# Order and padding of SBUF tiles in a two-layer decoder trunk in float32r

## The chip, the cores and the metric

The kernel runs on one core of a Trainium2 chip. The metric is the device time of one execution in microseconds (us). A core has a matrix engine (TensorE: PE in the profile, PEld for its weight loads), VectorE (DVE), ScalarE (ACT), GpSimd (POOL) and SyncE (SP); data come from HBM by DMA into SBUF, a memory of 128 partitions, and products go to PSUM. An address below is the offset in bytes within each partition of SBUF.

## The reference

Two layers over 256 tokens of width 2,048. Layer 0 has causal attention with 16 heads (the sequence is one MoBA block, so no past blocks are gathered), layer 1 a sliding window of 128 with four shared K/V heads and sinks. Each layer then has a gated FFN with a causal convolution of width 3, and each half ends in a layer norm over a scaled residual.

```python
def conv_ffn(x, w_up, conv_w, conv_b, w_down):
    h = x @ w_up                                   # [256, 2 * 5504]
    hc = conv_width_3(h, conv_w) + conv_b
    g, v = jnp.split(hc, 2, axis=-1)
    return (jax.nn.gelu(g) * v) @ w_down
...
for layer in range(2):
    attn = moba_attention(...) if layer == 0 else swa_attention(...)
    h = layer_norm(ALPHA * h + attn, ln_g[layer, 0], ln_b[layer, 0])
    ffn = conv_ffn(h, ffn_w_up[layer], ffn_conv_w[layer], ffn_conv_b[layer], ffn_w_down[layer])
    h = layer_norm(ALPHA * h + ffn, ln_g[layer, 1], ln_b[layer, 1])
```

Everything is float32.

## The kernel before

**Products in two parts.** A float32 operand is split into a high part in float32r and a low part, the rest (L84 and L85 for weights: ACT copies `raw` to `wh`, DVE subtracts to `wl`). A product is then three float32r products: high with high, high with low, low with high. Activations are kept in the same way, both parts in one tile: a block `k` of `xT`, `oT` or `aT` has 512 columns, the high part of 256 tokens and then the low part.

**The stream of weights.** All weights come as one stream of 709 halves of [128, 1024] float32, 512 KB each, in the order of use. `load_weights` (L65) issues a load on SP into one of four `raw` buffers, `split_upto` (L73) splits a half into one of four pairs `wh`/`wl`, three halves ahead of the products.

**Two kinds of products.** `ws_unit` (L194) makes a [128 features, 256 tokens] tile: per block of 128 rows, 128 columns of `wh` are stationary and all 512 columns of `xT[:, k]` move (L223), then 128 columns of `wl` are stationary and the 256 columns of the high part move (L224). It serves Q and K and the FFN's up-projection (86 units in each FFN, of which the first has another form, L207 to L212, with only 256 columns moving). `Moving` (L227) has 128 columns of the activations stationary, and a block of 512 columns of weights moves (L243 to L245): V, the attention's output projection (`src` is `oT`) and the FFN's down-projection (`aT`). All these products are float32r. Attention itself (L384, L385, L418, L419 and the transposes L411) and the transposes L324 are float32.

**Weights in xT.** In the last window of each `project_out`, xT is free, and four halves of weights (`aside`, L77 to L79) are split into xT instead of `wh`/`wl`: there both parts of a moving block are pieces of xT, 2,048 bytes long.

**Places.** A pool takes its place when it is opened, and a tile's buffers follow each other within it in the order of the calls, each rounded up to 32 bytes. The first 16,512 bytes hold the DMA ring and four constants. Then come `const` (L50: xT at 16,512, res, ident, eps, sk, nsk, junk), `wpool` (raw from 66,368), `spool` (wh from 82,752, wl from 99,136), `stat` (L55: small tiles, four buffers each, and `stats`), `gbp` (gb at 116,608), and from 132,992 on the pool of the stage, `att0`, `ffn0`, `att1` or `ffn1`, each opened when the one before is closed. In `att0` the order is xc, rb, oh, us, bias, oT (170,432), vt, qT, kT, L, PT; in `att1` bias, oT (149,376), vt, kT, qT, L, PT; in an FFN aT (132,992), cw, c0, c1, h. The pools end below 229,376, which is the end of a partition.

**Order of the work.** It is written out by hand: `at(n, f)` puts f ahead of the products of the n-th slot (a half) from now, `pe_at` behind them. SP's queue has the weight loads, POOL's the small loads, among them `cw` (L511), `band` and `bias` (L188, L192) and `gb` (L293); `layer_attention` (L435) sets the loads of bias to slots 4 and on.

Of the kernel before, what the change touches and what calls it, by code (L numbers as in the profile page):

```python
# [11 lines left out]
F32 = mybir.dt.float32  # L12
F32R = mybir.dt.float32r
# [4 lines left out]
P = 128  # L18
T = 256
D = 2048  # L20
KB = D // P
NH = 16
# [4 lines left out]
NCH = D // 512  # L27
# [3 lines left out]
ALPHA = math.sqrt(2.0)  # L31
# [15 lines left out]
def trunk(ctx: ExitStack, tc: tile.TileContext, wst, xT_in, x_in, relb, onehot, umask, sinks, conv_in, ln_g, ln_b, out):  # L47
    nc = tc.nc
    ctx.enter_context(tc.manual_schedule())
    const = ctx.enter_context(tc.tile_pool(name="const", bufs=1))  # L50
    wpool = ctx.enter_context(tc.tile_pool(name="wpool", bufs=RAW_BUFS))
    spool = ctx.enter_context(tc.tile_pool(name="spool", bufs=HALF_BUFS))
    psum = ctx.enter_context(tc.tile_pool(name="psum", bufs=4, space=bass.MemoryType.PSUM))
    dram = ctx.enter_context(tc.tile_pool(name="dram", bufs=1, space=bass.MemoryType.DRAM))
    stat = ctx.enter_context(tc.tile_pool(name="stat", bufs=4))  # L55
    gbp = ctx.enter_context(tc.tile_pool(name="gbp", bufs=1))

    n_halves = wst.shape[0]
    raws, halves, aside = {}, {}, {}
# [13 lines left out]
    def split_upto(i):  # L73
        while todo["split"] <= min(i, n_halves - 1):
            s = todo["split"]
            r = raws.pop(s)
            if s in aside:  # L77
                j = aside.pop(s)
                wh, wl = (xT[:, k:k + 2, :].rearrange("p a b -> p (a b)") for k in (4 * j, 4 * j + 2))  # L79
            else:  # L80
                wh = spool.tile([P, HW], F32R, name="wh")
                wl = spool.tile([P, HW], F32R, name="wl")
            for c in pieces(s):
                nc.scalar.activation(wh[:, c], r[:, c], AF.Copy)  # L84
                nc.vector.tensor_tensor(out=wl[:, c], in0=r[:, c], in1=wh[:, c].bitcast(F32), op=ALU.subtract)  # L85
            halves[s] = (wh, wl)
            todo["split"] += 1
            load_weights()

    slot = {"now": 0}  # L90
    before, behind = {}, {}

    def at(n, f, *a, first=False):
        """f runs n slots (halves of a unit of weights) from now, ahead of that slot's products."""
        fs = before.setdefault(slot["now"] + n, [])
        fs.insert(0 if first else len(fs), (f, a))

    def pe_at(n, f, *a):
        """f runs n slots from now, behind that slot's products."""
        behind.setdefault(slot["now"] + n, []).append((f, a))  # L100

    def run(agenda):
# [4 lines left out]
    def step():  # L107
        run(behind)
        slot["now"] += 1
# [3 lines left out]
    def take(ahead=AHEAD):  # L113
        i = nexth["i"]
        nexth["i"] += 1
        split_upto(i + ahead)
        run(before)
        return halves.pop(i)

    xT = const.tile([P, KB, 2 * T], F32R, name="xT")  # L120
    res = const.tile([P, 2, D], F32, name="res")

    def load_input(pool):
        xc = pool.tile([P, KB, T], F32, name="xc", bufs=1)
# [67 lines left out]
        nc.gpsimd.dma_start(bias[:, h0:h1, :], band[l, h0:h1].rearrange("h q j -> q h j"))  # L192

    def ws_unit(acc, feed=None):  # L194
        """acc[:, :T] += acc[:, T:] is x @ w, transposed. With feed, acc[:, :T] alone, with the
        products with the low part of x last: feed(k) readies the high part of block k, feed(KB)
        the low parts."""
        def cols(w, j):
            return w[:, j * P:(j + 1) * P]

        o = acc[:, 0:T]
        if feed:
            pair = [take(1 - i) for i in range(2)]
            for k in range(KB):
                feed(k)
                wh, wl = pair[k // 8]
                nc.tensor.matmul(o, cols(wh, k % 8), xT[:, k, 0:T], start=(k == 0), stop=False)  # L207
                nc.tensor.matmul(o, cols(wl, k % 8), xT[:, k, 0:T], start=False, stop=False)
            feed(KB)
            split_upto(nexth["i"] + AHEAD - 2)  # L210
            for k in range(KB):
                nc.tensor.matmul(o, cols(pair[k // 8][0], k % 8), xT[:, k, T:2 * T], start=False, stop=(k == KB - 1))  # L212
                if k % 8 == 7:
                    step()
                    split_upto(nexth["i"] + AHEAD - 2 + (k + 1) // 8)
                    if k < 8:
                        run(before)
            return
        for hf in range(2):
            wh, wl = take()  # L220
            for j in range(8):
                k = hf * 8 + j
                nc.tensor.matmul(acc, cols(wh, j), xT[:, k, :], start=(k == 0), stop=False)  # L223
                nc.tensor.matmul(o, cols(wl, j), xT[:, k, 0:T], start=False, stop=(k == KB - 1))  # L224
            step()

    class Moving:  # L227
        """Products with the weights as the moving operand, block after block of [128, 512]."""

        def __init__(self, src, nk):  # L230
            self.src, self.nk, self.half, self.pos = src, nk, None, 0
# [13 lines left out]
            nc.tensor.matmul(acc, sl, wh, start=False, stop=(k == self.nk - 1))  # L245

        def tilewise(self, accs, k, n, done):
            """Blocks k .. k+n, all of which the buffers hold, for one token tile after the other;
            done(t, i) is called behind half i of tile t."""
            blocks = []  # L250
            for t in range(2):
                for i in range(n):
                    if t == 0:
                        blocks.append(self.block(min(AHEAD, n // 2 - 1 - i // 2)))
                    self.mm(accs[t], k + i, t, *blocks[i])
                    if i % 2:
                        if t:
                            step()
                        done(t, i // 2)
                        if t:  # L260
                            run(before)

        def chunk(self, accs, early=None, late=None):
            """One chunk of 512 columns; early and late are the `done` of its first and its last
            blocks, done for one token tile after the other."""
            k = 0
            if early:
                k = 2 * HALF_BUFS
                self.tilewise(accs, 0, k, early)
            last = WINDOW_BLOCKS if late else 0  # L270
            while k < self.nk - last:
                wh, wl = self.block()
                for t in range(2):
                    self.mm(accs[t], k, t, wh, wl)
                k += 1
                if self.pos % 2 == 0:
                    step()
            if late:
                self.tilewise(accs, k, last, late)
# [2 lines left out]
        return psum.tile([P, 512], F32, name="acc")  # L282

    def project_out(src, nk, li, after, preload):
        """res = layer_norm(ALPHA * res + src @ w); its transpose goes to xT, split. For tile 1 the
        last steps, over chunks of columns, are returned."""
        mv = Moving(src, nk)
        w0 = nexth["i"] + (nk * NCH - WINDOW_BLOCKS) // 2
        aside.update({w0 + j: j for j in range(SPARE)})
        stats = stat.tile([P, 2, NCH, 6], F32, name="stats", bufs=1)  # L290
        gb = gbp.tile([P, 2, D], F32, name="gb")
        for i, a in enumerate((ln_g, ln_b)):
            nc.gpsimd.dma_start(gb[:, i], bass.AP(tensor=a.tensor, offset=a.offset + li * D, ap=[[0, P], [1, D]]))  # L293
# [77 lines left out]
        return lambda c: norm(1, c), (lambda c: turn(1, c), lambda c, pt: low(1, c, pt))  # L371

    def attention(pool, l, h, qT, vt, kT, bias, oT):
        """Softmax attention of head h, from the slot after the one that completes q^T."""
        at_tile = lambda: psum.tile([P, 512], F32, name="at")
        L = pool.tile([P, 3 * P], F32, name="L", bufs=3)
        PT = pool.tile([P, 3 * P], F32, name="PT", bufs=3)
# [2 lines left out]
        tiles = ((0, slice(0, P)), (1, slice(P, 3 * P)))  # L380
# [53 lines left out]

    def layer_attention(l, rest):  # L435
        with tc.tile_pool(name=f"att{l}", bufs=2) as pool:
            if l == 0:
                load_input(pool)
                bias_table(pool)
            else:  # L440
                nc.vector.tensor_scalar(nsk, sk, -1.0, None, op0=ALU.mult)
            bias = pool.tile([P, NH, 2 * P], F32, name="bias", bufs=1)
            for i, h in enumerate(range(0, NH, 4)):
                at(4 + (8 - 4 * l) * i, spread_bias, l, h, h + 4)
                at(4 + (8 - 4 * l) * i, load_bias, bias, l, h, h + 4)
            oT = pool.tile([P, NH, 2 * T], F32R, name="oT", bufs=1)

            def v_group(early=None):
                mv = Moving(xT, KB)
# [23 lines left out]
            if l == 0:  # L473
                for g in range(NH // 4):
                    vt = v_group()
                    for j in range(4):
                        h = 4 * g + j
                        q = feat_unit("qT", 4)
                        k = feat_unit("kT", 4)
                        attention(pool, l, h, q, vt[:, :, j * P:(j + 1) * P], k, bias, oT)  # L480
            else:
# [19 lines left out]
                for h in range(NH):  # L501
                    q = feat_unit("qT", 4)
# [73 lines left out]


def _still(w):
    """[K, N] as tiles of 128 columns, in two halves of K."""
    k, n = w.shape  # L580
    return w.reshape(2, k // P // 2, P, n // P, P).transpose(3, 0, 2, 1, 4).reshape(n // P, 2, P, HW)


def _moving(w):
    """[K, N] as blocks of [128, 512], two side by side, chunk of columns after chunk."""
    k, n = w.shape
    b = w.reshape(k // P, P, n // 512, 512).transpose(2, 0, 1, 3).reshape(-1, 2, P, 512)
    return b.transpose(0, 2, 1, 3).reshape(-1, P, HW)
# [59 lines left out]
```

## Time and profile before

| | |
|---|---|
| device time, median of 3 runs (lowest, highest) | 2143.48 us (2142.07, 2143.63) |
| span of the profiled execution, first to last instruction | 2143.1 us |
| its mean granted clock | 0.993 |
| PE, PEld, DVE, ACT, POOL busy | 99%, 84%, 67%, 46%, 1% |
| moved by DMA | 405.08 MB, 189 GB/s on the mean |

The profile is one execution taken by the hardware profiler. A matmul's busy time runs from its start to a modelled end, and consecutive matmuls overlap; the distance between two starts is what one costs in a full row of them. The granted clock is TensorE's, as a share of 2.4 GHz: 1.00, or 0.50 (1.2 GHz). A stage given with its bounds has, per engine, busy us and the number of instructions. The chain of waits goes back from the last instruction to what released each one.

### The profile page before, as it was taken

The numbers are of one execution on the slowest core, as the hardware profiler recorded it, in microseconds if no ns is written. First come the engines' busy times: TensorE is split into PE (matmuls) and PEld (weight loads), VectorE is DVE, ScalarE is ACT, GpSimd is POOL, SyncE is SP. The second block draws the span as 40 slices with busy tenths as digits, with TensorE's granted clock in tenths as the row PEclk, the third lists the DMA queues.
The fourth block names the chain that finished last, engine by engine and source line by source line (L and its number), as shares of the span: only waits on it lengthen the run. The fifth ranks groups of instructions, "written<-read, shape, count | busy, mean of one in ns | idle before, by whom it ended". The sixth has DMA issues, their size and how long they took to land.

```text
span 2143.1 us, 28513 instructions
## 1 busy us (share of the span) xinstructions
PE 2113.8 (99%) x10962; PEld 1792.8 (84%) x10962; DVE 1435.0 (67%) x2104; ACT 987.6 (46%) x1395; POOL 25.5 (1%) x40
## 2 busy tenths in 40 slices
PE   8999999999999999999999999999999999999997
PEld 7888888788888888888887888888888888888886
DVE  5555555787787777744456676687787778754445
ACT  5444444354544444433344554354444454443342
POOL 1100000000000000000001000000000000000000
PEclk9999999999999999999999999999999999999999
DMA  8855556455555555555556544565555555555553
GB/s 278 295 171 174 169 167 204 174 196 189 186 188 183 188 186 187 186 188 189 189 200 201 212 147 158 176 209 188 187 187 183 190 185 185 184 190 190 187 186 128
DMA packets 114120, 405.08 MB, mean 189 GB/s; under 512 B 15504, under 2 KB 15808, under 8 KB 112704
## 3 DMA queue, kind: packets, MB, share of 16 engines
q1 hardware_dynamic: 106848, 383.83, 53.4%
q0 software_dynamic: 7136, 19.44, 2.6%
q8 instruction: 86, 1.41, 0.3%
q14 instruction: 50, 0.41, 0.1%
HBM read 401.02 MB, written 6.34 MB: 190 GB/s over the span
## 4 chain that ended last, share of the span: by engine, by line
PE 97%; DVE 2%; DMA 0%; ACT 0%; issue 0%; SPq 0%; ACTq 0%
PE acc L223 39%; PE acc L224 20%; PE acc L244 12%; PE acc L245 12%; PE acc L243 12%; PE at L385 1%; PE at L418 1%; PE at L411 0%; DVE wl L85 0%; PE at L324 0%; PE at L384 0%; DMA raw<-in_wst_dram 0%; PE at L419 0%; DVE res L315 0%; DVE res L314 0%; ACT wh L84 0%
## 5 line engine op out<-in xcount | busy, mean ns | idle before, releaser
L85 DVE TENSOR_TENSOR wl<-raw,wh 128x1024 fp32r<-128x1024 f32 (+1 forms) x709 | 865.2, 1222 | 626.0 <-ACT wh L84 625.5
L223 PE MATMUL acc<-xT,wh 128*128 128x512 f32 x3552 | 1262.4, 397 | 0.0
L84 ACT ACTIVATE wh<-raw 128x1024 fp32r<-128x1024 f32 (+1 forms) x709 | 750.4, 1059 | 953.4 <-PE acc L245 353.1
L224 PE MATMUL acc<-xT,wl 128*128 128x256 f32 x3552 | 1000.9, 282 | 0.0
L223 PEld LDWEIGHTS acc<-xT,wh 128*128 128x128 f32 x3552 | 667.6, 188 | 159.2
L224 PEld LDWEIGHTS acc<-xT,wl 128*128 128x128 f32 x3552 | 667.1, 188 | 0.9
L243 PE MATMUL acc<-wh,aT 128*128 128x512 f32 x656 | 259.7, 396 | 0.0
L245 PE MATMUL acc<-wh,aT 128*128 128x512 f32 x656 | 259.4, 395 | 0.0
L244 PE MATMUL acc<-wl,aT 128*128 128x512 f32 x656 | 259.4, 395 | 0.0
L245 PEld LDWEIGHTS acc<-wh,aT 128*128 128x128 f32 x656 | 123.3, 188 | 29.7
L243 PEld LDWEIGHTS acc<-wh,aT 128*128 128x128 f32 x656 | 123.3, 188 | 29.6
L244 PEld LDWEIGHTS acc<-wl,aT 128*128 128x128 f32 x656 | 123.3, 188 | 29.5
L243 PE MATMUL acc<-wh,oT 128*128 128x512 f32 x224 | 90.1, 402 | 0.0
L245 PE MATMUL acc<-wh,oT 128*128 128x512 f32 x224 | 88.5, 395 | 0.0
L244 PE MATMUL acc<-wl,oT 128*128 128x512 f32 x224 | 88.4, 395 | 0.0
L534 DVE SCALAR_TENSOR_TENSOR c<-h,cw,c 128x255 f32<-128x255 f32 x170 | 82.3, 484 | 6.0
L535 DVE SCALAR_TENSOR_TENSOR c<-h,cw,c 128x254 f32<-128x254 f32 x170 | 82.1, 483 | 6.1
L243 PE MATMUL acc<-wh,xT 128*128 128x512 f32 x160 | 67.1, 419 | 7.9 <-ACT wh L84 7.9
L533 DVE TENSOR_SCALAR c<-h,cw 128x256 f32<-128x256 f32 x170 | 70.3, 414 | 6.1
L532 DVE TENSOR_TENSOR h<-acc,h 128x256 f32<-128x256 f32 x170 | 70.9, 417 | 0.0
L244 PE MATMUL acc<-wl,xT 128*128 128x512 f32 x160 | 65.4, 409 | 1.5 <-DVE wl L85 1.3
L541 ACT ACTIVATE aT<-c 128x256 fp32r<-128x256 f32 x86 | 36.0, 419 | 66.4 <-DVE c L538 66.4
(102 smaller groups left out, 1199.3 us busy)
## 6 DMA issues: line engine op xcount, KB each, us to landing
raw<-in_wst_dram SPq DMA_DIRECT2D x723, 512.0 KB, 3.3
band<-ud POOLq DMA_DIRECT2D x8, 512.0 KB, 12.8
bias<-band POOLq DMA_DIRECT2D x8, 512.0 KB, 5.5
gb<-in_ln_g_dram POOLq DMA_DIRECT2D x4, 1024.0 KB, 6.3
gb<-in_ln_b_dram POOLq DMA_DIRECT2D x4, 1024.0 KB, 9.0
res<-in_x_dram POOLq DMA_DIRECT2D x2, 1024.0 KB, 9.7
out_dram<-res SPq DMA_DIRECT2D x8, 256.0 KB, 2.5
xc<-in_xT_dram SPq DMA_DIRECT2D x7, 256.0 KB, 7.4
```

What stands on the lines that cost most here:

```text
L84: nc.scalar.activation(wh[:, c], r[:, c], AF.Copy)
L85: nc.vector.tensor_tensor(out=wl[:, c], in0=r[:, c], in1=wh[:, c].bitcast(F32), op=ALU.subtract)
L223: nc.tensor.matmul(acc, cols(wh, j), xT[:, k, :], start=(k == 0), stop=False)
L224: nc.tensor.matmul(o, cols(wl, j), xT[:, k, 0:T], start=False, stop=(k == KB - 1))
L243: nc.tensor.matmul(acc, sh, wh, start=(k == 0), stop=False)
L244: nc.tensor.matmul(acc, sh, wl, start=False, stop=False)
L245: nc.tensor.matmul(acc, sl, wh, start=False, stop=(k == self.nk - 1))
L532: nc.vector.tensor_tensor(out=h, in0=acc[:, 0:T], in1=h, op=ALU.add)
L533: nc.vector.tensor_scalar(c, h, w[:, 2:3], w[:, 3:4], op0=ALU.mult, op1=ALU.add)
L534: nc.vector.scalar_tensor_tensor(c[:, 1:T], h[:, 0:T - 1], w[:, 1:2], c[:, 1:T], op0=ALU.mult, op1=ALU.add)
L535: nc.vector.scalar_tensor_tensor(c[:, 2:T], h[:, 0:T - 2], w[:, 0:1], c[:, 2:T], op0=ALU.mult, op1=ALU.add)
L541: nc.scalar.activation(aT[:, i, 0:T], g, AF.Copy)
```

## The change

Only places change, no instruction. xT and res leave `const` for a pool `big` of their own, opened behind `stat`, which moves ahead of the large pools; `stats` is padded from 6 to 10 elements per entry, 128 bytes in all; and in the attention pools oT and bias are taken first, in this order. The docstrings of several functions are blanked, with the line count kept.

```diff
     const = ctx.enter_context(tc.tile_pool(name="const", bufs=1))
+    stat = ctx.enter_context(tc.tile_pool(name="stat", bufs=4))
+    big = ctx.enter_context(tc.tile_pool(name="big", bufs=1))
     wpool = ctx.enter_context(tc.tile_pool(name="wpool", bufs=RAW_BUFS))
     spool = ctx.enter_context(tc.tile_pool(name="spool", bufs=HALF_BUFS))
     psum = ctx.enter_context(tc.tile_pool(name="psum", bufs=4, space=bass.MemoryType.PSUM))
     dram = ctx.enter_context(tc.tile_pool(name="dram", bufs=1, space=bass.MemoryType.DRAM))
-    stat = ctx.enter_context(tc.tile_pool(name="stat", bufs=4))
     gbp = ctx.enter_context(tc.tile_pool(name="gbp", bufs=1))
...
-    xT = const.tile([P, KB, 2 * T], F32R, name="xT")
-    res = const.tile([P, 2, D], F32, name="res")
+    xT = big.tile([P, KB, 2 * T], F32R, name="xT")
+    res = big.tile([P, 2, D], F32, name="res")
...
-        stats = stat.tile([P, 2, NCH, 6], F32, name="stats", bufs=1)
+        stats = stat.tile([P, 2, NCH, 6], F32, name="stats", bufs=1, padded_shape=[P, 2, NCH, 10])
...
         with tc.tile_pool(name=f"att{l}", bufs=2) as pool:
+            oT = pool.tile([P, NH, 2 * T], F32R, name="oT", bufs=1)
+            bias = pool.tile([P, NH, 2 * P], F32, name="bias", bufs=1)
             if l == 0:
                 load_input(pool)
                 bias_table(pool)
             else:
                 nc.vector.tensor_scalar(nsk, sk, -1.0, None, op0=ALU.mult)
-            bias = pool.tile([P, NH, 2 * P], F32, name="bias", bufs=1)
             for i, h in enumerate(range(0, NH, 4)):
...
-            oT = pool.tile([P, NH, 2 * T], F32R, name="oT", bufs=1)
```

## Rows read from the trace of the kernel before

**Rows 1.** The page, busy us (share of the span) xinstructions of each engine.
```profile
PE 2113.8 (99%) x10962; PEld 1792.8 (84%) x10962; DVE 1435.0 (67%) x2104; ACT 987.6 (46%) x1395; POOL 25.5 (1%) x40
```

**Rows 2.** The chain of waits, whole span, shares by line.
```profile
by line: PE acc L223 38.7%; PE acc L224 19.8%; PE acc L244 11.8%; PE acc L245 11.7%; PE acc L243 11.7%; PE at L385 0.6%; PE at L418 0.6%; PE at L411 0.5%; DVE wl L85 0.5%; PE at L324 0.4%; PE at L384 0.4%; DMA raw<-in_wst_dram 0.3%; PE at L
```

**Rows 3.** Matmul groups by line and shape: xcount | busy us, mean ns | idle before.
```profile
L223 PE MATMUL acc<-xT,wh 128*128 128x512 f32 x3552 | 1262.4, 397 | 0.0
...
L243 PE MATMUL acc<-wh,aT 128*128 128x512 f32 x656 | 259.7, 396 | 0.0
...
L243 PE MATMUL acc<-wh,oT 128*128 128x512 f32 x224 | 90.1, 402 | 0.0
...
L243 PE MATMUL acc<-wh,xT 128*128 128x512 f32 x160 | 67.1, 419 | 7.9 <-ACT wh L84 7.9
```

**Rows 4.** Timeline of PE, FFN up-projection, layer 0: start us, us; first and last.
```profile
700.16 0.28 PE L224 MATMUL acc<-xT,wl 128*128 128x256 f32 x1
...
705.81 0.28 PE L224 MATMUL acc<-xT,wl 128*128 128x256 f32 x1
```

**Rows 5.** Timeline of PE, beside attention, layer 0: first and last.
```profile
61.21 0.28 PE L224 MATMUL acc<-xT,wl 128*128 128x256 f32 x1
...
65.75 0.28 PE L224 MATMUL acc<-xT,wl 128*128 128x256 f32 x1
```

**Rows 6.** Timeline of PE, FFN down-projection, layer 0: first and last.
```profile
1060.03 0.40 PE L244 MATMUL acc<-wl,aT 128*128 128x512 f32 x1
...
1066.33 0.39 PE L244 MATMUL acc<-wl,aT 128*128 128x512 f32 x1
```

**Rows 7.** Stage (span, busy by engine, PEclk, DMA), then chain, under the lower clock.
```profile
405.00:408.00 3.00, 3.00 (x16) 3.00 (x15) 2.60 (x5) 0.67 (x2) 1.60 (x3) 0.50 0.31 46
...
405.07 0.21 PE acc L208
```

**Rows 8.** Timeline of PE, weights in xT: layer 0, then layer 1's two token tiles.
```profile
374.74 0.39 PE L243 MATMUL acc<-xT,oT 128*128 128x512 f32 x1
...
379.41 0.39 PE L245 MATMUL acc<-xT,oT 128*128 128x512 f32 x1
...
1372.85 0.39 PE L243 MATMUL acc<-xT,oT 128*128 128x512 f32 x1
...
1377.38 0.39 PE L245 MATMUL acc<-xT,oT 128*128 128x512 f32 x1
...
1384.59 0.39 PE L243 MATMUL acc<-xT,oT 128*128 128x512 f32 x1
...
1387.99 0.39 PE L243 MATMUL acc<-xT,oT 128*128 128x512 f32 x1
```

**Rows 9.** The first two of these stretches, busy us by engine, PEclk, DMA share, GB/s.
```profile
374.74:379.40 4.66, 4.66 (x21) 3.76 (x20) 4.62 (x6) 1.58 (x2) 0.00 (x0) 1.00 0.25 75
1372.85:1377.39 4.54, 4.54 (x22) 3.76 (x21) 4.51 (x6) 1.50 (x2) 0.00 (x0) 1.00 0.19 63
```

**Rows 10.** Chain of waits, first unit of each FFN, in order of time.
```profile
410.95 1.88 PE acc L212 x16
...
1408.24 1.81 PE acc L212 x16
```

**Rows 11.** One stage of the up-projection, then the page's GB/s in 40 slices.
```profile
500.00:600.00 100.00, 100.00 (x568) 87.03 (x568) 78.91 (x125) 49.90 (x71) 0.00 (x0) 1.00 0.55 184
...
GB/s 278 295 171 174 169 167 204 174 196 189 186 188 183 188 186 187 186 188 189 189 200 201 212 147 158 176 209 188 187 187 183 190 185 185 184 190 190 187 186 128
```

**Rows 12.** Timeline of POOL, then of DVE: last load of bias, first use.
```profile
1174.98 0.78 POOL L192 DMA_DIRECT2D bias<-band  x1 [16.08 <-DMA band<-ud]
...
1199.38 0.28 DVE L389 SCALAR_TENSOR_TENSOR L<-at,bias 128x128 f32<-128x128 f32 x1
```

**Rows 13.** Timeline of PE, project_out of layer 0: first and last.
```profile
340.12 0.40 PE L244 MATMUL acc<-wl,oT 128*128 128x512 f32 x1
...
345.00 0.40 PE L244 MATMUL acc<-wl,oT 128*128 128x512 f32 x1
```

## The prediction

> **What bounds the kernel now.** I read the page's busy line first, then the chain of waits by line, then the matmul groups with shapes kept apart, then start times. PE is busy for 99% of the span [rows 1], and the chain is made of the products of L223, L224 and L243 to L245 almost alone [rows 2]. So only what changes the distance from one matmul's start to the next, or what makes PE wait anew, can move the time. "Busy" does not show that distance, because matmuls overlap (L223 has a mean of 397 ns and 3,552 of them [rows 3] would be 1,410 us); start times do. Three patterns carry the time:
> - FFN up-projection, L223 (512 moving columns) and L224 (256) in turn: 16 pairs in 5.65 us, 353 ns a pair [rows 4].
> - The same pairs beside attention: 13 pairs in 4.54 us, 349 ns [rows 5].
> - L243 to L245, always 512 columns: 27 starts in 6.30 us, 233.3 ns each [rows 6].
>
> How much is that above what the columns need? While the granted clock was at its lower level (0.50, 1.2 GHz), a matmul of 256 columns took 0.21 us on the chain, 256/1.2 = 213 ns, nothing over [rows 7]. At the full clock (1.00, 2.4 GHz) the same count would be 107 ns, 512 columns 213 ns, a pair 320 ns. So a pair loses 29 to 33 ns and a 512-column product 20 ns, only at the full clock.
>
> **Does an operand's address decide that loss?** The addresses follow from the pools' order and the tiles' sizes (each rounded up to 32 bytes). Before, with the first 16,512 bytes taken, xT lies at 16,512, wh and wl from 82,752 and 99,136 on, aT at 132,992, oT at 170,432 in layer 0 and at 149,376 in layer 1. Their remainders by 128 are 0 for xT, aT and layer 1's oT, and 64 for wh, wl and layer 0's oT. The trace holds an experiment on this. Near the end of each project_out four halves of weights are put into xT instead of wh and wl, so the same code moves xT against oT in both layers. Layer 1 (remainders 0 and 0): 20 starts in 4.53 us, 226.5 ns, and for the second token tile 15 in 3.40 us, 226.7. Layer 0 (0 and 64): 20 starts in 4.67 us, 233.5 ns [rows 8]. Clock, DVE and ACT were alike beside them, and DMA was light in both [rows 9]. The products that move wh (64) against aT (0) have 233.3 [rows 6]. So where both operands start at multiples of 128 the product costs 6.6 ns less. An address does matter.
>
> It isn't all. The 16 products of L212 (256 columns) in each FFN's first unit have the same addresses in both layers, and took 1.88 us in one and 1.81 us in the other, 118 and 113 ns [rows 10]; likewise the pairs with 353 and 349 [rows 4, 5]. So the chain has states that it can fall into at one set of addresses. The best ones agree: 113.3 is half of 226.6. I take these as what aligned operands give: a pair would be 226.6 + 113.3 = 340 ns.
>
> The Trainium skill says otherwise. Its page "TensorE: Matmul & The Clock Gate", section "What happens when you issue a matmul", has TensorE read moving operand and weights through two independent ports, so that a weight load takes nothing from a running product, and by "Back-to-back issue gap" 512 columns take some 216 ns wherever they lie. By that the change gives nothing; rows 8 speak against it, 233.3 is not 216, and it is rival C.
>
> **The change part by part.** No instruction is added or removed. After, the constants end at 17,216, the small tiles take 1,088 + 128 (the padding) and end at 18,432 = 9 x 2,048; xT, res, raw, wh, wl, gb, and then oT or aT follow, each a multiple of 2,048 long. So every float32r operand does lie as the title says. Slices of 128 columns of a stationary tile lie at multiples of 512.
>
> *Pairs.* 3,552 [rows 3], of which 2 x (86 - 1) units x 16 = 2,720 are in the FFNs and 832 beside attention. wh and wl go from remainder 64 to 0; xT stays at 0. FFN: 353.1 - 340 = 13.1 ns x 2,720 = 35.6 us. Attention: states of 349 to 353 are mixed there, mean about 350.5: 10.5 ns x 832 = 8.7 us. Bounds: the pair could stay (0), or lose everything down to 320 ns (33 ns x 2,720 + 30.5 x 832 = 115 us), or go the other way (rival D). I take 340, the sum of the two rows nearest to it, hence 44.3 us.
>
> *512-column products with wh or wl moving.* (656 + 224 + 160) x 3 = 3,120 [rows 3]. 233.3 - 226.6 = 6.7 ns x 3,120 = 20.9 us. Bounds: 0, and down to 213 ns, 20 ns x 3,120 = 62 us. I take 6.7 ns, which is measured on the same shapes.
>
> *fp32 products* (L324, L384 to L419). In layer 0 vt starts at 203,328, no multiple of 2,048, and ident stays at 16,512: here the title does not hold. They have some 2.5% of the chain [rows 2], 54 us; a change like that of the pairs (4%) would be 2 us either way. I take 0.
>
> *DVE, ACT, DMA.* DVE is busy for 79 of 100 us in the up-projection; a faster PE makes that 79 of some 96 us, and even 10% longer instructions would leave it at 87. DMA goes from 184 GB/s to 191, where the first slices moved 278 and 295 [rows 11]. So both stay hidden: 0. If DVE did set the pace, the pairs' 44 us would not come, which is rival B's time.
>
> *Places that change hands.* In the layer pools, oT and bias now lie below xc and the table's tiles, so each lies over other old tiles. POOL's queue waits there: layer 1's last bias load started at 1174.98 us, and the first use of bias is at 1199.38 [rows 12], 24 us later. Old readers (project_out) and new writers stand in the same order as before, so I cost this at 0; if the loads came some us later it would still be 0, and beyond the 24 us it would be the excess. The strided stats tile is read by eight short DVE instructions: 0.
>
> Sum: 44.3 + 20.9 = 65 us. The profiled execution spans 2143.1 us; its median with what lies around it is 2143.48, 0.4 more. 2143.1 - 65.2 + 0.4 = 2078.
>
> **The rivals.**
> A (forecast): both patterns reach the best state. 2 ns either way on a pair is 7 us, 1 ns on a product 3 us, the attention mix 2 us: 2066 to 2090. Chance 0.45.
> B: the wh-moving products gain, the pairs do not or only reach 349. For it: pairs had an aligned xT all along, and L212 changed state without any address. Against: their weights had remainder 64. Time: 2143.5 - 20.9 = 2123, with 349 in the FFNs (4.1 ns x 2,720 = 11 us) 2111. Chance 0.19.
> C: the position as such decides nothing (the ports are independent, the two layers' difference is a state): 2143, within 0.2%, which is about what a measurement of this kernel can tell from no change. Rows 8 and 9 are against it. Chance 0.12.
> D (slower): moving and stationary data now start at the same offset within 512 bytes, which no row has: in the fast rows they are 256 apart (xT 128, oT 384). If both streams then meet in the same place at the same time, each weight load costs the product beside it more. It decides from the point where a 512-column product needs over 233.3 ns. Price, taken as the present loss over the fast state once more: 13.1 x 3,552 + 6.7 x 3,120 = 67 us, 2211. For it: products of wh against layer 0's oT, both at remainder 64, had 21 starts in 4.88 us, 232.4 ns [rows 13], so that like remainders alone do not make a product fast. Against: layer 1's two token tiles were equally fast [rows 8], with stationary slices at 1,920 and 896 for one and 384 and 1,408 for the other, so a shift by 512 does no harm. Chance 0.14.
> E: all loss goes. 115 + 62 us less gives 1966; half of it 2055. Nothing at full clock shows it for float32r. Chance 0.10.
>
> **How the numbers follow.** Faster: A + B + E = 0.74; same: C = 0.12; slower: D = 0.14. The range takes A, B, C and the nearer half of E, 0.81: 2025 to 2146; A's own is 2066 to 2090.
>
> **What would show it.** L243 to L245 moving wh start every 226.7 ns: the second term holds; 233 again: C; 240: D. Pairs at 340 ns: the first term; 349 or 353: B; over 366: D. The L212 group at 1.81 us in both layers supports A. The sum is wrong if PE gains a wait on wh or wl, or if DVE's share in 500 to 600 us passes 90% with PE waiting.

## The result and the profile after

The changed kernel takes 2124.85 us (median of 4 runs, 2124.57 to 2125.27), the kernel before 2143.56; the ratio is 0.9917, with a 95% interval of 0.9903 to 0.9931. The forecast was 2078: the sign was right, and 18.7 of 65 us came. That is close to rival B's time, 2123. Over all the experiments the kernel before never took less than 2130.04 us, 5 us above the changed kernel. What the prediction calls "the title" is this: every float32r tile starts at a multiple of 2,048 bytes.

All lines below have numbers one higher than before, so L224 and L225 are the pairs and L244 to L246 the products that move weights. First the matmul groups, by shape, to set beside [rows 3].

```profile
L224 PE MATMUL acc<-xT,wh 128*128 128x512 f32 x3552 | 1262.9, 401 | 0.0
...
L244 PE MATMUL acc<-wh,aT 128*128 128x512 f32 x656 | 255.7, 390 | 0.0
...
L244 PE MATMUL acc<-wh,oT 128*128 128x512 f32 x224 | 89.0, 398 | 0.0
...
L244 PE MATMUL acc<-wh,xT 128*128 128x512 f32 x160 | 65.9, 412 | 8.3 <-ACT wh L85 8.1 <-ACT xT L327 0.2
```

The counts are the same; by busy time a product with aT is 6 ns shorter, and L224 is 4 ns longer. The starts in the timeline say it better: two of the down-projection, to set beside [rows 6], then two of the up-projection, beside [rows 4].

```profile
1054.93 0.39 PE L246 MATMUL acc<-wh,aT 128*128 128x512 f32 x1
...
1061.05 0.39 PE L246 MATMUL acc<-wh,aT 128*128 128x512 f32 x1
```

```profile
700.05 0.28 PE L225 MATMUL acc<-xT,wl 128*128 128x256 f32 x1
...
705.71 0.28 PE L225 MATMUL acc<-xT,wl 128*128 128x256 f32 x1
```

27 starts in 6.12 us are 226.7 ns each, where it was 233.3. 16 pairs in 5.66 us are 354 ns each, where it was 353: nothing came of them. Added over the span, from one start to the next, L244 to L246 take 764.1 us against 784.2, which is 20.1 us less, and L224 with L225 take 1260.6 against 1260.3. The span of the profiled execution went from 2143.1 to 2123.0 us. So one term of the sum came whole, and the other not at all.

The rest stands as it was. The chain has the first unit's short products, [rows 10] before, now equal in both layers and longer; a stage of the up-projection answers to [rows 11], POOL and DVE to [rows 12], and PE's waits are led by 8.1 us, in three waits, on ACT's split of the weights, where it was 7.9 us.

```profile
406.20 1.92 PE acc L213 x16
...
1394.48 1.92 PE acc L213 x16
```

```profile
500.00:600.00 100.00, 100.00 (x567) 86.78 (x567) 79.13 (x125) 49.27 (x70) 0.00 (x0) 1.00 0.58 189
```

```profile
1163.92 0.78 POOL L193 DMA_DIRECT2D bias<-band  x1 [13.11 <-DMA band<-ud]
...
1186.78 0.28 DVE L390 SCALAR_TENSOR_TENSOR L<-at,bias 128x128 f32<-128x128 f32 x1
```

### The profile page after: what moved, and what is told of

The parts are those of the page before. It is cut to its first block, busy times and chain, and to the rows that moved or that the text cites. A ratio compares the mean times of both kernels' runs of the same rounds, so it can differ in the third digit from the quotient of the medians.

```text
span 2123.0 us, 28513 instructions
## 1 busy us (share of the span) xinstructions
PE 2092.1 (99%) x10962; PEld 1785.8 (84%) x10962; DVE 1434.8 (68%) x2104; ACT 987.6 (47%) x1395; POOL 25.5 (1%) x40
## 4 chain that ended last, share of the span: by engine, by line
PE 97%; DVE 2%; ACT 0%; DMA 0%; issue 0%; SPq 0%; ACTq 0%; DVEq 0%
PE acc L224 39%; PE acc L225 20%; PE acc L245 11%; PE acc L246 11%; PE acc L244 11%; PE at L386 1%; PE at L419 1%; DVE wl L86 1%; PE at L412 0%; PE at L385 0%; DMA raw<-in_wst_dram 0%; PE at L420 0%; DVE xT L332 0%; DVE res L316 0%; DVE res L315 0%; PE at L325 0%
## 5 line engine op out<-in xcount | busy, mean ns | idle before, releaser
L224 PE MATMUL acc<-xT,wh 128*128 128x512 f32 x3552 | 1262.9, 401 | 0.0
L225 PE MATMUL acc<-xT,wl 128*128 128x256 f32 x3552 | 997.5, 281 | 0.0
L224 PEld LDWEIGHTS acc<-xT,wh 128*128 128x128 f32 x3552 | 667.8, 188 | 163.7
L225 PEld LDWEIGHTS acc<-xT,wl 128*128 128x128 f32 x3552 | 671.7, 189 | 0.9
L244 PE MATMUL acc<-wh,aT 128*128 128x512 f32 x656 | 255.7, 390 | 0.0
L246 PE MATMUL acc<-wh,aT 128*128 128x512 f32 x656 | 255.4, 389 | 0.0
L245 PE MATMUL acc<-wl,aT 128*128 128x512 f32 x656 | 255.4, 389 | 0.0
L246 PEld LDWEIGHTS acc<-wh,aT 128*128 128x128 f32 x656 | 123.1, 188 | 25.6
L244 PEld LDWEIGHTS acc<-wh,aT 128*128 128x128 f32 x656 | 123.2, 188 | 25.5
L245 PEld LDWEIGHTS acc<-wl,aT 128*128 128x128 f32 x656 | 123.2, 188 | 25.4
L244 PE MATMUL acc<-wh,oT 128*128 128x512 f32 x224 | 89.0, 398 | 0.0
L246 PE MATMUL acc<-wh,oT 128*128 128x512 f32 x224 | 87.4, 390 | 0.0
L245 PE MATMUL acc<-wl,oT 128*128 128x512 f32 x224 | 87.3, 390 | 0.0
L244 PE MATMUL acc<-wh,xT 128*128 128x512 f32 x160 | 65.9, 412 | 8.3 <-ACT wh L85 8.1
L245 PE MATMUL acc<-wl,xT 128*128 128x512 f32 x160 | 64.1, 400 | 1.5 <-DVE wl L86 1.5
```

The lines of the kernel that those rows point to most:

```text
L244: nc.tensor.matmul(acc, sh, wh, start=(k == 0), stop=False)
L245: nc.tensor.matmul(acc, sh, wl, start=False, stop=False)
```

## The experiments

Each is the changed kernel or the kernel before with one edit. Distance means the start of the moving operand less that of the stationary one, by 256 bytes. The theories:

- T1: each operand has to start at a multiple of 128 bytes (the forecast's reading).
- T2: only the distance counts.
- P1: a pair stays slow because long and short products alternate, as the weight load beside the short one has too little time. T5 is what became of it behind e1: after a short product a row of long ones has to settle.
- P2 and T3: a pair too follows its distance, whatever the order.
- T4: in a pair the alternation sets the pace, whatever the distance.

**What makes a product of 512 columns fast.** e3 moves everything by 64 bytes.

```diff
+    shift = big.tile([P, 16], F32, name="shift")
+    nc.gpsimd.memset(shift, 0.0)
     xT = big.tile([P, KB, 2 * T], F32R, name="xT")
```

> The changed kernel with 64 bytes ahead of xT, so that xT, wh, wl, oT and aT all lie at remainder 64 by 128, and still at the same remainder by 2,048 as each other. Theory T1 (each operand has to start at a multiple of 128): the products that move weights go back to 231 to 233.3 ns, 3,120 x 4.5 to 6.7 = 14 to 21 us, so 2139 to 2146. Theory T2 (only the distance of moving and stationary operand counts): they stay at 226.7 and the time at 2125.

2124.90 us, the time of the changed kernel to 0.1 us. The down-projection's starts (28 of them, the first and the last):

```profile
1055.00 0.39 PE L247 MATMUL acc<-wl,aT 128*128 128x512 f32 x1
...
1061.12 0.39 PE L247 MATMUL acc<-wl,aT 128*128 128x512 f32 x1
```

226.7 ns with every operand at remainder 64 by 128. T1 has fallen. e4 starts at the other end: multiples of 128, but at other distances.

```diff
+    pad1 = ctx.enter_context(tc.tile_pool(name="pad1", bufs=1)).tile([P, 16], F32, name="pad1")
...
     wpool = ctx.enter_context(tc.tile_pool(name="wpool", bufs=RAW_BUFS))
...
     gbp = ctx.enter_context(tc.tile_pool(name="gbp", bufs=1))
+    pad2 = gbp.tile([P, 16], F32, name="pad2")
...
```

> The kernel before with two pads of 64 bytes, ahead of raw and ahead of the layers' pools: wh and wl then lie at remainder 384 by 512, aT and layer 1's oT at 0, xT as before at 128; layer 0's oT stays at remainder 64 by 128. So all but layer 0's oT start at multiples of 128, but not of 256 or 2,048, and wh and aT are 128 apart by 256. T1: products of wh with aT, layer 1's oT and xT at 226.7 ns, with layer 0's oT at 233: 2,784 x 6.7 = 18.7 us, so 2125. T2 in the form that the distance has to be a multiple of 256: wh with aT and oT stays at 233, 2139 to 2144.

2139.41 us. First wh and wl against aT (distance 128), then against layer 0's oT (distance 64), first and last of 28 and 22 starts:

```profile
1054.93 0.40 PE L248 MATMUL acc<-wl,aT 128*128 128x512 f32 x1
...
1061.20 0.40 PE L248 MATMUL acc<-wl,aT 128*128 128x512 f32 x1
```

```profile
339.86 0.39 PE L247 MATMUL acc<-wh,oT 128*128 128x512 f32 x1
...
344.67 0.39 PE L247 MATMUL acc<-wh,oT 128*128 128x512 f32 x1
```

232.2 and 229.0 ns: two operands at multiples of 128 were slower than two of which only one was. With all runs together (medians of three successive products of L243 to L245, wherever they stand in a kernel, a third each), each distance has its own number:

| distance by 256 | ns per product of 512 | seen with |
|---|---|---|
| 0 | 226.7 | before: xT with aT; after and e3: all; e4: wh with xT |
| 64 | 229.0 | e4: wh with layer 0's oT; e6: wh with xT; e14: xT with aT |
| 128 | 231.7 to 232.0 | before: wh with layer 0's oT; e4: wh with aT; e5: xT with aT |
| 192 | 233.3 to 234.0 | before: wh with aT; e6: xT with aT; e7 and e14: wh with xT |

At 128 the products of one row differ, and their mean is higher than the median, 232.4 (e4, wh with aT) to 233.1 ns (e5, xT with aT); so over a row 128 and 192 are nearly alike. T2 holds, tried in steps of 64 bytes, and neither 2,048 nor 128 is the number. In these rows the stationary operand in use and the next one, which is loaded beside it, have the same remainder, so the runs don't tell which of the two counts. e14 takes that to the change itself: the kernel before, with oT and aT alone moved to wh's remainder of 64.

```diff
     gbp = ctx.enter_context(tc.tile_pool(name="gbp", bufs=1))
+    pad2 = gbp.tile([P, 48], F32, name="pad2")
...
         with tc.tile_pool(name=f"att{l}", bufs=2) as pool:
+            oT = pool.tile([P, NH, 2 * T], F32R, name="oT", bufs=1)
+            bias = pool.tile([P, NH, 2 * P], F32, name="bias", bufs=1)
...
```

> The kernel before with one part of the change alone: oT and bias first in the attention pools, and 192 bytes ahead of the layers' pools, so that oT and aT share their remainder by 256 with wh and wl (64); xT, raw, wh and wl stay where they were. By the distance: wh with oT and aT at 226.7, 2,640 x 6.7 = 17.7 us; wh with xT and xT with oT/aT (192 and 64 by 256) about as before; pairs as before (353.3, at times 349): 2126, and less if the pairs fall to 349 for longer. By absolute multiples of 2,048: no gain, 2143.

2126.54 us, against 2124.85 for the whole change: this part alone gives 17.0 of the 18.7 us.

```profile
1054.87 0.39 PE L245 MATMUL acc<-wh,aT 128*128 128x512 f32 x1
...
1060.98 0.39 PE L245 MATMUL acc<-wh,aT 128*128 128x512 f32 x1
```

27 starts in 6.11 us, 226.3 ns.

**Why the pairs did not follow.** e1 changes the order in the changed kernel, e2 in the kernel before.

```diff
             for j in range(8):
                 k = hf * 8 + j
                 nc.tensor.matmul(acc, cols(wh, j), xT[:, k, :], start=(k == 0), stop=False)
+            for j in range(8):
+                k = hf * 8 + j
                 nc.tensor.matmul(o, cols(wl, j), xT[:, k, 0:T], start=False, stop=(k == KB - 1))
```

> The changed kernel, with the products of ws_unit in another order: for each half first the eight products of 512 columns (high weights), then the eight of 256 columns (low weights). Nothing is added or left out. Theory P1 (the pair's loss comes from the alternation: a weight load that is followed by the short product has too little time beside it): rows of 512 cost 226.7 ns each as in L244 to L246, rows of 256 cost 113 to 120 ns, a pair 340 to 347 instead of 353.3; 3,552 pairs give 22 to 47 us, so 2078 to 2103. Theory P2 (the loss comes from where xT and wh lie against each other, whatever the order): a pair stays near 353, the time within 3 us of 2125.

> The kernel before, with the same new order of the products in ws_unit. P1 with an effect of alignment on top: rows of 512 with the weights at remainder 64 by 128 cost 233.3 ns, rows of 256 113 to 120, a pair 347 to 353; 2122 to 2143. P1 without any effect of alignment in these products: the same pair as in the aligned kernel, 340 to 347, so 2097 to 2122. P2: no change, 2143.5.

e1: 2110.16 us, ratio to the kernel before 0.9849 (0.983 to 0.9868). e2: 2115.04 us in one run. Order alone is worth 15 us on the changed kernel and 28 on the kernel before, which is more than that kernel's whole spread, so P2 has fallen; but e1's pair is 349 ns on the mean, not the 340 to 347 that P1 gave, and e2's, at the distance of 64, is 345, shorter than e1's, which neither form of P1 had. The timeline of e1 shows where its pair loses. Each line merges like neighbours: a row of eight long products from its start, the same row from its sixth product, the short row behind it, and the next long one.

```profile
698.73 2.00 PE L224 MATMUL acc<-xT,wh 128*128 128x512 f32 x8
...
699.89 0.61 PE L224 MATMUL acc<-xT,wh 128*128 128x512 f32 x2
...
700.57 1.11 PE L227 MATMUL acc<-xT,wl 128*128 128x256 f32 x8
701.53 2.00 PE L224 MATMUL acc<-xT,wh 128*128 128x512 f32 x8
```

The first five long ones take 1.16 us, 232 ns each, the last three 0.68 us, 226.7 each. So at distance 0 the stream has to settle behind a short product, five products long, and only then runs at the pace that its distance gives. The eight short ones take 0.96 us, 120 ns. In a pair every long product has a short one before it.

e12 tests it from the other side: order, addresses and weight loads of the changed kernel, but L225 takes 512 columns too.

```diff
-                nc.tensor.matmul(o, cols(wl, j), xT[:, k, 0:T], start=False, stop=(k == KB - 1))
+                nc.tensor.matmul(acc, cols(wl, j), xT[:, k, :], start=False, stop=(k == KB - 1))
```

> The changed kernel with L225 taking all 512 columns of xT like L224 (it adds the product of the two low parts, which the kernel leaves out). Order, addresses and weight loads are the same. T5 (the change of length is what keeps the pairs from settling): all products at 226.7, a pair 453.3, 3,552 x 100 = 355 us more than the changed kernel, 2480. If instead the change from wh to wl or ws_unit's operands themselves cost, 230 to 233 a product: 2503 to 2525.

2482.23 us.

```profile
699.73 0.39 PE L224 MATMUL acc<-xT,wh 128*128 128x512 f32 x1
...
706.98 0.39 PE L224 MATMUL acc<-xT,wh 128*128 128x512 f32 x1
```

16 pairs in 7.25 us: 453.1 ns, 226.6 a product, where the other reading gave 460 to 466. With all lengths equal, the pairs' operands at distance 0 are as fast as the down-projection's. So it takes the short product to keep a pair at 353. Two things come with it, the change of length and the shorter time for the weight load beside it, and e12 does not part them. In e1's rows the first five long products are slow although the load beside each, which starts within 5 ns of it, has a long product's time; that speaks against the load's time as the whole cause.

e5 and e6 leave the pairs in their order and move xT alone, to 128 and 192 above wh and wl, in the changed kernel (ident, sk and nsk go behind xT, and `stats` loses its padding, so that the rest keeps its remainder).

```diff
+    pad0 = big.tile([P, 32], F32, name="pad0")      # 48 in e6
...
     xT = big.tile([P, KB, 2 * T], F32R, name="xT")
+    ident = big.tile([P, P], F32, name="ident")     # from const, with sk and nsk
...
+    pad1 = big.tile([P, 64], F32, name="pad1")      # 48 in e6
...
```

> The changed kernel with xT alone moved: it lies 128 by 256 above wh and wl, which still share their remainder with oT and aT. Order of the products as before. Theory T3 (a pair's cost too follows the distance of moving and stationary operand by 256): a pair is away from 353.3 by 2 ns or more, the time by 7 us or more from 2125. Theory T4 (in a pair the change between the long and the short product sets the pace, whatever the distance): 352 to 354, the time 2125 to 2127 (the four halves in xT and the V products, 160 x 3 with the distance reversed, lose some 5 ns each, 2 us).

> As e5 with a distance of 192 by 256. T3: a pair away from 353.3 by 2 ns or more. T4: 352 to 354, 2125 to 2128.

2120.59 and 2129.28 us. Pairs of e5, then of e6:

```profile
700.05 0.40 PE L228 MATMUL acc<-xT,wh 128*128 128x512 f32 x1
...
705.31 0.40 PE L228 MATMUL acc<-xT,wh 128*128 128x512 f32 x1
```

```profile
699.92 0.28 PE L229 MATMUL acc<-xT,wl 128*128 128x256 f32 x1
...
705.92 0.28 PE L229 MATMUL acc<-xT,wl 128*128 128x256 f32 x1
```

15 pairs in 5.26 us, 351 ns, and 17 in 6.00 us, 353. Neither theory holds as it was worded. e6's pairs stay at 353.3, as T4 had it, though its time is 1.3 us above T4's range; e5's are at 351.1 on the mean of the FFNs, 2.2 ns off, as T3 had it, and its time, 4 us below the changed kernel's, lies outside both ranges. Three of the four distances give 353 (64 in the kernel before, 0 and 192), and 128 gives 2 ns less.

e7 and e8 have e1's order, with xT 64 and 128 above wh and wl (e5's edit with 16 and 32 columns in pad0, 80 and 64 in pad1).

> Order split per half as in e1, and xT 64 by 256 above wh and wl, as it lay in the kernel before; wh, wl, oT and aT share their remainder. If distance alone decides within a row of like products, the pair is that of e2 (229.5 + 115.8 = 345 ns) and the products of wh with aT and oT that of e1 (226.7): 2115 - 2,640 x 6.7 ns = 2097. If the absolute place counts too, the pair is nearer to e1's 350 and the time nearer to 2110.

> As e7 with a distance of 128 by 256. By the runs so far a row of 512 columns at this distance costs 231.7 to 232.7 ns (wh with aT in e4); if the short products stay at 116 to 120 a pair is 348 to 353 and the time 2107 to 2126. If the short products gain by the distance (120 at 0, 116 at 64), they are at 112 to 114 and the pair at 344 to 347, 2093 to 2104.

2099.34 and 2123.20 us. e7 came out as distance alone would have it: two rows of e7,

```profile
701.18 1.11 PE L231 MATMUL acc<-xT,wl 128*128 128x256 f32 x8
702.12 2.00 PE L228 MATMUL acc<-xT,wh 128*128 128x512 f32 x8
703.96 1.07 PE L231 MATMUL acc<-xT,wl 128*128 128x256 f32 x8
```

0.94 us for eight short ones and 1.84 for eight long ones, 117 and 230 ns. Over both FFNs e7's first five long products are no slower than its last three, 229 ns on the mean, so nothing settles at this distance. Then e8:

```profile
701.83 1.12 PE L231 MATMUL acc<-xT,wl 128*128 128x256 f32 x8
702.78 2.02 PE L228 MATMUL acc<-xT,wh 128*128 128x512 f32 x8
704.64 1.10 PE L231 MATMUL acc<-xT,wl 128*128 128x256 f32 x8
```

0.95 us for eight short ones and 1.86 for eight long ones, 119 and 233 ns, so the second guess there was wrong. A pair is 351 ns, the same as e5's: at a distance of 128 the order is worth nothing. e7 beats both kernels. Run again with an interval:

> The kernel of e7 once more, with its interval: 2099, 2.1% under the kernel before and 1.2% under the changed one.

2098.98 us (2097.35 to 2100.49, 4 runs), ratio 0.9801 (0.9782 to 0.9819).

**Longer rows.** e9 to e11 have rows of sixteen, a whole unit, with both halves taken ahead of the short products (e9 on the changed kernel, e10 with xT 64 higher, e11 with wl alone 192 higher).

```diff
+        pair = []
         for hf in range(2):
-            wh, wl = take()
+            pair.append(take(AHEAD - hf))
             for j in range(8):
                 k = hf * 8 + j
-                nc.tensor.matmul(acc, cols(wh, j), xT[:, k, :], start=(k == 0), stop=False)
-                nc.tensor.matmul(o, cols(wl, j), xT[:, k, 0:T], start=False, stop=(k == KB - 1))
-            step()
+                nc.tensor.matmul(acc, cols(pair[hf][0], j), xT[:, k, :], start=(k == 0), stop=False)
+            if hf == 0:
+                step()
+        for k in range(KB):
+            nc.tensor.matmul(o, cols(pair[k // 8][1], k % 8), xT[:, k, 0:T], start=False, stop=(k == KB - 1))
...
+        step()
```

and for e11

```diff
+    lpool = ctx.enter_context(tc.tile_pool(name="lpool", bufs=HALF_BUFS))
+    pad2 = lpool.tile([P, 48], F32, name="pad2", bufs=1)
...
-                wl = spool.tile([P, HW], F32R, name="wl")
+                wl = lpool.tile([P, HW], F32R, name="wl")
```

> The changed kernel (all at multiples of 2,048), with the products of a whole unit in two rows: sixteen of 512 columns, then sixteen of 256. Theory T5 (at a distance of 0 the first five long products behind a short one are slow, 233, 236, 229, 232, 231 ns, and only then does the row settle at 226.7; a pair has a short one each time and so never settles): (1161 + 11 x 226.7)/16 = 228.4 for a long one and 119.5 for a short one, a pair 348 against 350 in rows of eight; 2125 - 3,552 x 5.3 ns = 2106. If instead the rows of eight had slow products for another reason (the stationary slices beyond 2,048 of a half), the slow ones come back in the second half of the row and the time stays at 2110.

> As e9, with xT 64 by 256 above wh and wl. A long product at this distance goes on at 229 (no settling to 226.7), a short one at 113 or 118: a pair 345 and 2097 to 2100, as in rows of eight; or, if a longer row of short products stays at 113 once it is there, 342 and 2089.

> As e9, with wl alone moved up by 192: wh, xT, oT and aT share their remainder by 256, and xT lies 64 above wl. Long products as in e9, 228.4, short ones 116: a pair 344, 32 us less than the changed kernel. L245 (wl moving) now has a distance of 192 in a row of three with two of 0: if each product follows its own distance, 1,040 x 6.7 = 7 us more, so 2100; if one such product in three keeps the row from settling, up to 233 for all, 21 us more, so 2114.

2152.09, 2152.54 and 2156.72 us: all three miss. Between two rows of sixteen PE waits, as e9's timeline shows:

```profile
700.87 2.07 PE L229 MATMUL acc<-xT,wl 128*128 128x256 f32 x16
703.18 3.93 PE L225 MATMUL acc<-xT,wh 128*128 128x512 f32 x16 [0.24 <-ACT wh L85]
```

Fifteen short products at 120 and the last would end at 702.79; the next long one starts 0.39 us later, behind ACT's copy of its weights. A half's buffers are now held until the short products at the end of the unit, and the splits behind them come late. So these times say nothing on what longer rows are worth. The traces do answer two questions of these runs. The first: do e9's slow products come back in the second half of its row? From the seventh of the same sixteen on, as the timeline shows it:

```profile
704.67 2.43 PE L225 MATMUL acc<-xT,wh 128*128 128x512 f32 x10
...
706.94 2.07 PE L229 MATMUL acc<-xT,wl 128*128 128x256 f32 x16
```

Ten in 2.27 us, 227.0 ns each: they don't, so it isn't the place of a slice within its half. The second: does one product in three at distance 192 hold up the other two? e11's down-projection has wl there and wh at 0.

```profile
1070.08 0.39 PE L256 MATMUL acc<-wl,aT 128*128 128x512 f32 x1
...
1076.26 0.39 PE L256 MATMUL acc<-wl,aT 128*128 128x512 f32 x1
```

27 starts in 6.18 us, 228.9 ns, which is the mean of 226.7, 226.7 and 233.3: among equal lengths the prices of the distances add up.

**The spread of the kernel before.** Some of its runs were faster than the others, so it was timed again, unchanged.

> The kernel before, unchanged, for its spread. If the pairs' state (353.3 or 349) is drawn anew in each execution, some times lie between 2130 and 2143.5, as 2,720 pairs x 4.3 ns = 12 us would have it, and none far below; if the two low times came from elsewhere, none does here.

Ten runs from 2130.04 to 2144.57 us, median 2140.95, ratio to the same kernel 0.999 (0.9972 to 1.0008); the changed kernel's four lay within 0.7 us. The times lie where pairs at 353 or 349 would put them, but no low run was profiled: in the profiled execution of 2141.7 us the pairs were at 353.3 ns in the FFNs. It differs from the one shown before in the granted clock beside the second layer norm (1136 to 1146 us), 1.00 where that had 0.81. First the kernel before as first profiled, then as profiled here:

```profile
1136.00:1146.00 10.00, 7.24 (x23) 4.65 (x22) 6.83 (x11) 3.95 (x6) 1.40 (x2) 0.81 0.76 234
```

```profile
1136.00:1146.00 10.00, 6.89 (x31) 4.80 (x30) 7.40 (x12) 4.28 (x6) 1.90 (x2) 1.00 0.73 223
```

For all that, the two spans, 2141.7 and 2143.1 us, differ by 1.4 us only. And the mean clocks of the ten runs do not go with their times: the runs of 2130.04 and 2143.55 us both had 0.996, those of 2138.00 and 2144.57 both 0.994. So the clock does not explain the 14 us, and what does stays open.

## Why the prediction was wrong

- **What bounds the kernel**: right. Only the distances between starts moved, and no engine or queue came onto the path.
- **The products that move wh and wl**: 20.9 us forecast, 20.1 measured, 226.7 ns a product as forecast.
- **The pairs**: the step that failed. 44.3 us were forecast, none came (0.3 us the other way). The prediction took "the best ones agree: 113.3 is half of 226.6" as what aligned operands give, and added the pace of a row of long products to that of a row of short ones. e1 shows that a row at distance 0 needs five long products to reach its pace, and e12 that a pair of equal lengths at the same addresses does reach it; a pair of unequal ones does not, at any of the four distances (351 to 353). What the short product does to the long one stays open. The short row did not give 113 either: at distance 0 it went to 120 (1.92 us for sixteen, in both layers), the opposite of what was to support the forecast. The mean of 350.5 beside attention was low, too: over all pairs there it is 351.3.
- **Why an address matters**: the measured 226.7 and 233.3 were read as remainders by 128. It is the distance by 256 (e3, e4, e14). That the down-projection's forecast held, though its reason did not, is because the change makes this distance 0 as well; that was luck. The rows read before had a hint: wh against layer 0's oT, with like remainders by 128, was slow [rows 13], and the prediction put that down to rival D.
- **Rival D**: its fear, the same offset within 512, is not borne out; 0 and 256 by 512 are alike.
- **Rival B**: right in its time and in which products gain, with a chance of 0.19. Its ground, that xT was aligned all along, is not the cause: e5 and e6 move xT, and the pairs gain 2 ns at the most.
- **Rival C** and the page behind it: the Trainium skill's "TensorE: Matmul & The Clock Gate", section "What happens when you issue a matmul", has two independent read ports. e3, e4 and e14 only move tiles (and fill a pad), and a product costs 226.7 to 233.3 ns by the distance of its two operands, so for float32r at the full clock the place of the stationary operand changes what the moving one costs. Whether it is at the ports that they meet, no run shows.
- **The terms at 0** (float32 products, DVE, DMA, POOL's waits): right. Layer 1's last load of bias still starts 23 us ahead of its first use, and DVE's share in the up-projection is 79%.

## What to carry to other kernels

When matmuls stand back to back, read the distance between starts in the trace and set it against the columns; where one shape shows two values, look for what differs in the addresses of its two operands against each other, not for round numbers. A pace that is measured in a row of like products does not hold for a mixture: before adding up two rows, look whether the trace has the mixture at the better pace anywhere. Here the order of the products (like lengths together, half by half) was worth 15 us at one distance, 28 at another and nothing at a third, so the two have to be tried together; the best pair of them gave 2099 us.

## What the runs showed of the hardware

- A float32r product of 512 columns at the full clock costs 226.7, 229.0, 232.4 to 233.1 or 233.3 ns on the mean with its moving operand 0, 64, 128 or 192 bytes (by 256) above its stationary one, in rows of equal lengths. Steps below 64 bytes weren't tried.
- The pace depends on what went before: at distance 0 five products of 232 ns on the mean before 226.7 (e1), at 64 no such start (e7). Rows of 256 columns run at 113 to 118 ns at a distance of 64 and at 120 at a distance of 0.
- In turn, 512 and 256 columns cost 353 ns a pair at distances 0, 64 and 192 and 351 at 128; in rows of eight 349, 345 and 351 at 0, 64 and 128. What meets in SBUF there, and why five, no run shows.
